# A decoder layer in split fp32: new start addresses, modulo 256 bytes, for the operands of the feed-forward matmuls

## The chip, the cores and the metric

The kernel runs as one program on one core of one Trainium2 chip. The metric is the time of one execution on the device, in microseconds (us). For the kernel before, the median of two runs is 1110.34 us (1110.25 and 1110.42).

## The reference

One decoder layer over 256 tokens of width 2048, in fp32. A mixer (attention over 8 heads beside a state-space branch) ends in a projection, a norm and a residual sum. Then comes the part that this case is about:

```python
h = rms_norm(x, ln_ffn_pre[l])
u = causal_depthwise_conv(h @ w_ffn_up[l], ffn_conv_w[l], ffn_conv_b[l])
gate, up = jnp.split(u, [FFN_HIDDEN], axis=-1)
f = (jax.nn.gelu(gate, approximate=True) * up) @ w_ffn_down[l]
x = x + rms_norm(f, ln_ffn_post[l])
```

`w_ffn_up` is 2048 x 11264 and `w_ffn_down` 5632 x 2048.

## The kernel before

**Split numbers.** A matmul in the fp32r type streams one column after the other but keeps fewer bits than fp32. So every operand is kept as two fp32r summands, `hi` and `lo` (the value minus `hi`), and a product is formed from three of the four partial products: hi*hi, hi*lo, lo*hi. TensorE (PE) does this work; everything else feeds it.

**Weights.** All weights come from HBM in units of 128 x 1024 fp32 (512 KB): 88 units of `win`, 32 of `wout`, and then twice 88 of `wup` and 44 of `wdown`. `Weights` (line 59) keeps them in rings. For each unit SyncE (SP) issues the load into a slot of `raw`, ScalarE (ACT) rounds it into a slot of `whi` (line 78) and VectorE (DVE) writes the difference into a slot of `wlo` (line 79). The rings of `whi` and `wlo` have 4 slots each in the pool `wp`; from the end of the mixer on, `deepen` adds 3 each in the pool `wq`. `tick` fetches one unit for each unit that PE has consumed.

**Projections by columns** (`cols_tile`, line 250, and `cols_part`, line 210), for the up projection: an output tile of 128 hidden columns by 256 tokens takes two units, each with 8 blocks of 128 x 128 weights. For each block `k` of the 16, the weights are the stationary operand and the activations `h2` the moving one, in a pair of matmuls:

```python
nc.tensor.matmul(ps, w[0][:, s], both, start=(k == 0), stop=False)
end[0] = nc.tensor.matmul(ps[:, c], w[1][:, s], hi, start=False, ...
```

The first (line 214) holds a block of `whi` and streams `both`, the two summands of `h2`, 2 x 256 columns; the second (line 215) holds the same block of `wlo` and streams the 256 columns of `hi`. Each loads its own stationary block (`LDWEIGHTS` in the profile's PEld rows). There are 88 such tiles; the first three of them (`held_up`) are worked in pieces by lines 223 and 226, so that 85 x 16 = 1360 pairs go by lines 214 and 215.

**Projections by rows** (`rows_chunk`, line 283, and `rows_part`, line 273), for the down projection: here a block of the gated activations `gT` is stationary and 512 columns of a weight unit stream. For each of the 22 blocks of a half, two token blocks and four chunks of 512 output columns there are three matmuls: `hi` with `whi` (line 278), `hi` with `wlo` (line 279), `lo` with `whi` (line 280), in all 6 x 176 = 1056 in the two halves.

**The feed-forward part** runs over two halves of the hidden width. In each half PE works 44 tiles of the up projection (22 gate tiles and 22 up tiles, in turn). ACT and DVE add the two halves of a finished sum in PSUM (`cols_sum`), apply the convolution, the GeLU and the product, and split the result into `gT` (`split_evac`). Then the four row chunks of the down projection over this half follow.

**Addresses.** SBUF addresses here are bytes within a partition, as the built program assigns them, and a residue is that address modulo 256. Every slot of `whi` and `wlo`, in `wp` and in `wq`, starts at residue 32. A block of 128 columns is 512 bytes and a chunk of 512 columns 2048, so every block and chunk in them starts at 32 as well. `normed` (line 340) makes `h2` as two planes, `lo` first, with 32 elements (128 bytes) beyond a plane's 4096: `lo` of each block `k` starts at 160 and `hi` at 32. `gT` is `[P, HALF, 2, S]` at residue 32, so every block of it, `hi` or `lo`, starts at 32. For the column projections of the mixer a shift (`SHIFT`, an argument of `units`) moves `wlo` by 128 bytes, to 160; there `hT` has its two summands side by side at 32. The row projections of the mixer have 32 against 32.

**Order.** The order on each engine is made by a scheduler from the order in which the code asks, its own estimates of when buffers come free, and the dependences.

Of the kernel before, what the change touches and what calls it, by code (L numbers as in the profile page):

```python
# [9 lines left out]
F32 = mybir.dt.float32  # L10
F32R = mybir.dt.float32r
# [3 lines left out]
ALU = mybir.AluOpType  # L15
# [4 lines left out]
P = 128  # L20
D = 2048
S = 256
# [7 lines left out]
HALF = NF // 2  # L30
# [3 lines left out]
UE = 1024  # L34
RELW = 384
RAWB = 4
SPLB = 4


SHIFT = 32  # L40
LOE = UE + 2 * SHIFT
HOLD = 5
MORE = {"raw": 0, "whi": 3, "wlo": 3}
WARM = 16
SIDE = 4

# [9 lines left out]
    return ap.bitcast(F32)  # L56


class Weights:

    def __init__(self, nc, pool, units):
        self.nc, self.pool, self.units = nc, pool, units
        self.fetched, self.ready, self.more, self.base, self.behind = 0, [], None, 0, 0

    def deepen(self, pool):

        self.more, self.base, self.behind = pool, self.fetched, MORE["whi"]

    def split(self, raw, hi, lo, i, s):
        self.rounded(raw, hi, lo, i, s)()
# [9 lines left out]
    def place(self, i, n, bufs, dtype):  # L82
        pool = self.pool
        if self.more and (i - self.base) % (bufs + MORE[n]) < MORE[n]:
            pool, bufs = self.more, MORE[n]
        wide = n == "wlo" and pool is self.pool
        return pool.tile([P, LOE if wide else UE], dtype, name=n, tag=n, bufs=bufs)
# [36 lines left out]
def decoder_layer(ctx, tc, x, xT, win, wdt, wout, wup, wdown, relb, vec, cols, mconv, fconv,  # L124
                  consts, out):
    nc = tc.nc
# [18 lines left out]
    def tok(t):  # L145
        return slice(t * P, (t + 1) * P)
# [63 lines left out]
    def cols_part(ps, w, aT, k, j):  # L210

        s = tok(j)
        both, hi, c = wide_and_hi(aT, k)
        nc.tensor.matmul(ps, w[0][:, s], both, start=(k == 0), stop=False)  # L214
        end[0] = nc.tensor.matmul(ps[:, c], w[1][:, s], hi, start=False,  # L215
                                  stop=(k == KT - 1)).ins

    def cols_tok(ps, w, aT, k, j, t):

        s = tok(j)  # L220
        both = ps.rearrange("p (b c) -> p b c", b=2)[:, :, tok(t)]
        c = k * S
        nc.tensor.matmul(both, w[0][:, s], aT[:, :, c:c + S][:, :, tok(t)],  # L223
                         start=(t == 0 and k == 0), stop=False)
        if t == NT - 1:
            nc.tensor.matmul(ps[:, S:], w[1][:, s], aT[:, 1, c:c + S], start=False,  # L226
                             stop=(k == KT - 1))

    def cols_sum(dst, ps):

        nc.scalar.copy(dst, ps[:, S:])
        nc.vector.tensor_tensor(dst, ps[:, :S], dst, op=ALU.add)

    pending, end = [], [None]

# [11 lines left out]
            with tc.issue_after(end[0]):  # L247
                fn(*args)

    def cols_tile(ps, aT):  # L250
        for u in range(2):
            w = ws.take()
            for j in range(8):
                cols_part(ps, w, aT, u * 8 + j, j)
            tick()

    def cols_first(pss, aT, after):
# [12 lines left out]
    def chunk_psums():  # L270
        return [acc.tile([P, 512], F32, name="pa", tag="a") for _ in range(NT)]
# [40 lines left out]
    def units(w, a, n, shift=0):  # L312
        return [(w[i], shift) for i in range(a, a + n)]

    ws = Weights(nc, wp, units(win, 0, 16, SHIFT) + units(win, 16, 16) + units(win, 32, 16, SHIFT)
                 + units(win, 48, 16) + units(win, 64, 24, SHIFT) + units(wout, 0, 32)
                 + [u for half in range(2)
                    for u in units(wup, half * 88, 88) + units(wdown, half * 44, 44)])
# [21 lines left out]
    def normed(name):  # L340

        return pers.tile([P, 2, KT * S + SHIFT], F32R, name=name, tag="h", bufs=1)

    def wide_and_hi(aT, k):

        if len(aT.shape) == 4:
            return aT[:, k, :, :], aT[:, k, 0, :], slice(0, S)
        c = slice(k * S, (k + 1) * S)
        return aT[:, :, c], aT[:, 1, c], slice(S, 2 * S)

    def summands(aT):

        if len(aT.shape) == 4:
            return [aT[:, :, c, :] for c in range(2)]
        return [aT[:, c, :KT * S].rearrange("p (k s) -> p k s", s=S) for c in (1, 0)]
# [5 lines left out]
    with ExitStack() as mctx:  # L361
# [3 lines left out]
        with ExitStack() as actx:  # L365
# [90 lines left out]
            rows = pers.tile([P, NT, SG, 8, P], F32, name="rows", tag="mm", bufs=1)  # L456
# [291 lines left out]
            lo, hi = range(8, KT, 2), range(0, 8, 2)  # L748
            first = [chunk_psums() for _ in range(2)]
# [25 lines left out]
        h2 = normed("h2")  # L775
# [38 lines left out]
        def turned(t, q):  # L814

            pt = psum("pxt").rearrange("p (j c) -> p j c", c=P)
            for j in range(4):
                nc.tensor.transpose(pt[:, j, :], ml[t][q][:, tok(j)], ident)
            dst = [d[:, q * 4:q * 4 + 4, tok(t)] for d in summands(h2)]
# [19 lines left out]
        both = list(lo) + list(hi)  # L839
# [111 lines left out]
    def summed(ps):  # L951
        u = fp.tile([P, S], F32, name="cfu", tag="cf", bufs=8)
        cols_sum(u, ps)
        return u

    def conv_ffn(f, u):
# [48 lines left out]
    def gated(i, ug, uu):  # L1005
        cg = conv_ffn(i, ug)
        nc.scalar.activation(cg, cg, AF.Gelu_apprx_tanh)
        cu = conv_ffn(NF + i, uu)
        k = i % HALF
        nc.vector.tensor_tensor(cu, cg, cu, op=ALU.mult)  # L1010
        split_evac(gT, k, slice(0, S), cu)

    held = []
    defer(5, lambda: along_tokens(rb2, [sums[:, t:t + 1] for t in range(NT)]))
    for half in range(2):
        for i in range(half * HALF, (half + 1) * HALF):
            ps = held_up[2 * i:2 * i + 2]
            for _ in range(2 - len(ps)):
                ps.append(col_psum())
                cols_tile(ps[-1], h2)  # L1020
            us = [summed(p) for p in ps]
            if i < 2:
                defer(5 - 2 * i, gated, i, *us)
            else:
                gated(i, *us)
        if half == 1:
            wpo = pers.tile([P, D], F32, name="wpo", tag="h", bufs=1)
            aux(out=wpo, in_=row_bcast(V_FFNPOST, D))
            nc.scalar.mul(wpo, wpo, -0.5)
        for c in range(4):  # L1030
            if half == 0 and c >= 2:
                held.append([psum("ph") for _ in range(NT)])
                rows_chunk(held[-1], gT, range(0, HALF, 2), last=False)
            elif half == 1 and c == 2:
                rows_chunk(held[0], gT, range(0, HALF, 2), first=False, done=fdone(1, c))
            elif half == 1 and c == 3:
                fearly += [early_sum(ss[2][t][:, :3]) for t in range(NT)]
                kts = range(0, HALF, 2)
                tail = rows_to_tail(held[1], gT, kts, first=False)
                for t in range(NT):  # L1040
                    for j in range(HOLD):
                        rows_tail(held[1], gT, kts, tail, t, j)
                    fdone(1, 3)(t, held[1][t])
            else:
                rows_chunk(chunk_psums(), gT, range(0, HALF, 2), done=fdone(half, c))


def _cols_units(w):
# [97 lines left out]
```

## Time and profile before

| | |
|---|---|
| median of the runs | 1110.34 us |
| the profiled execution, first to last instruction (its span) | 1107.4 us |
| the profiled execution as a whole, beside its span | not given by the profile; the median lies 2.9 us above the span |
| PE busy | 1100.1 us, 99% of the span |
| DVE, ACT busy | 784.0 us (71%), 592.3 us (53%) |
| granted TensorE clock, mean | 0.998 |
| matmuls by lines 214/215 with `h2` | 1360 + 1360 |
| matmuls by lines 278, 279, 280 with `gT` | 1056 |

The profile gives for each matmul a start and a modelled end. Matmuls overlap in the pipeline: a 128x512 one is shown as 0.39 us long, but the next one starts 0.23 us after it. So what a matmul costs is read from the distance between starts, which is called its pitch here, or from the count of matmuls in a window in which PE never waits. The times in a timeline are rounded to 0.01 us.

### The profile page before, as it was taken

Reading aid. Unit: us, or ns where it says so; the run is one execution under the profiler, and the core shown is the slowest. Engines: PE = TensorE matmul, PEld = TensorE weight load, DVE = VectorE, ACT = ScalarE, POOL = GpSimd, SP = SyncE. Lnnn points to the kernel's source line nnn. Section 1 sums busy time; section 2 is a strip of 40 time slices with the busy share of each in tenths; the row PEclk is TensorE's granted clock in tenths of the full one; section 3 lists DMA queues with packets and bytes.
Section 4 is the critical chain, followed back from the end, with each engine's and each line's share of the span. In section 5 each row is a group of like instructions: output and inputs, shape, how many; then the busy total and the mean of one; then the engine's idle time right before and its main releaser. Section 6 shows DMA issues by size and latency. Waiting matters only on the chain.

```text
span 1107.4 us, 15791 instructions
## 1 busy us (share of the span) xinstructions
PE 1100.1 (99%) x5888; PEld 945.1 (85%) x5888; DVE 784.0 (71%) x1270; ACT 592.3 (53%) x914; POOL 15.5 (1%) x26
## 2 busy tenths in 40 slices
PE   9999999999999999999999999999999999999997
PEld 7888888888888988888888888888888888888886
DVE  6698976776566899878787644448787878765553
ACT  6666545545454586555555444345555555554441
POOL 0010000000000000000000000000000000000000
PEclk9999999999999999999999999999999999999999
DMA  8857555555687267665556665565566565666652
GB/s 297 298 187 262 186 154 167 177 172 168 217 298 245 96 216 242 192 189 190 191 188 189 194 195 190 192 194 188 191 189 191 189 192 190 189 201 219 200 158 76
DMA packets 61356, 217.58 MB, mean 196 GB/s; under 512 B 7200, under 2 KB 8624, under 8 KB 60384
## 3 DMA queue, kind: packets, MB, share of 16 engines
q1 hardware_dynamic: 59328, 207.64, 58.3%
q0 software_dynamic: 1664, 8.59, 2.3%
q8 instruction: 46, 0.75, 0.3%
q10 hardware_dynamic: 288, 0.35, 0.1%
q14 instruction: 30, 0.25, 0.1%
HBM read 214.44 MB, written 2.11 MB: 196 GB/s over the span
## 4 chain that ended last, share of the span: by engine, by line
PE 99%; DMA 0%; SPq 0%; ACT 0%; issue 0%; DVE 0%; POOLq 0%; ACTq 0%
PE pa L214 36%; PE pa L215 18%; PE pa L278 9%; PE pa L280 9%; PE pa L279 9%; PE ph L280 4%; PE ph L279 4%; PE ph L278 4%; PE pab L214 1%; PE pa L223 1%; PE pab L215 1%; PE py L604 1%; PE pa L226 0%; PE pq L223 0%; DMA raw<-in_win_dram 0%; PE lg L694 0%
## 5 line engine op out<-in xcount | busy, mean ns | idle before, releaser
L79 DVE TENSOR_TENSOR wlo<-raw,whi 128x1024 fp32r<-128x1024 f32 (+2 forms) x389 | 469.7, 1210 | 249.0 <-ACT whi L78 240.9
L78 ACT CAST whi<-raw 128x1024 fp32r<-128x1024 f32 (+2 forms) x389 | 403.7, 1040 | 415.5 <-PE pa L214 193.3
L214 PE MATMUL pa<-h,whi 128*128 128x512 f32 x1360 | 471.7, 394 | 0.0
L215 PE MATMUL pa<-h,wlo 128*128 128x256 f32 x1360 | 379.4, 279 | 0.0
L214 PEld LDWEIGHTS pa<-h,whi 128*128 128x128 f32 x1360 | 255.7, 188 | 57.7
L215 PEld LDWEIGHTS pa<-h,wlo 128*128 128x128 f32 x1360 | 255.5, 188 | 0.0
L214 PE MATMUL pa<-hT,whi 128*128 128x512 f32 x384 | 136.5, 397 | 0.0
L215 PE MATMUL pa<-hT,wlo 128*128 128x256 f32 x384 | 107.0, 281 | 0.0
L214 PEld LDWEIGHTS pa<-hT,whi 128*128 128x128 f32 x384 | 72.1, 188 | 15.2 <-issue 0.2
L962 DVE SCALAR_TENSOR_TENSOR cfc<-cfu,fcv,cfc 128x254 f32<-128x254 f32 (+1 forms) x176 | 83.5, 479 | 1.4
L215 PEld LDWEIGHTS pa<-hT,wlo 128*128 128x128 f32 x384 | 72.1, 189 | 0.6 <-issue 0.2
L278 PE MATMUL pa<-whi,gT 128*128 128x512 f32 x176 | 68.6, 390 | 0.0
L280 PE MATMUL pa<-whi,gT 128*128 128x512 f32 x176 | 68.5, 389 | 0.0
L278 PE MATMUL ph<-whi,gT 128*128 128x512 f32 x176 | 68.5, 389 | 0.0
L279 PE MATMUL pa<-wlo,gT 128*128 128x512 f32 x176 | 68.5, 389 | 0.0
L279 PE MATMUL ph<-wlo,gT 128*128 128x512 f32 x176 | 68.5, 389 | 0.0
L280 PE MATMUL ph<-whi,gT 128*128 128x512 f32 x176 | 68.5, 389 | 0.0
L960 ACT ACTIVATE cfc<-cfu,fcv 128x256 f32<-128x256 f32 x88 | 52.3, 598 | 1.3 <-DVE cfu L959 1.3
L278 PE MATMUL pa<-whi,hT 128*128 128x512 f32 x128 | 51.2, 400 | 0.0
L278 PE MATMUL pa<-whi,mT 128*128 128x512 f32 x128 | 50.3, 393 | 0.0
L280 PE MATMUL pa<-whi,hT 128*128 128x512 f32 x128 | 50.1, 392 | 0.0
L279 PE MATMUL pa<-wlo,hT 128*128 128x512 f32 x128 | 50.0, 391 | 0.0
(230 smaller groups left out, 1131.6 us busy)
## 6 DMA issues: line engine op xcount, KB each, us to landing
raw<-in_wup_dram SPq DMA_DIRECT2D x176, 512.0 KB, 3.7
raw<-in_wdown_dram SPq DMA_DIRECT2D x88, 512.0 KB, 3.6
raw<-in_win_dram SPq DMA_DIRECT2D x85, 512.0 KB, 3.6
raw<-in_wout_dram SPq DMA_DIRECT2D x32, 512.0 KB, 3.9
xsq<-in_x_dram SPq DMA_DIRECT2D x2, 1024.0 KB, 10.3
rows<-acd POOLq DMA_DIRECT2D x4, 512.0 KB, 8.9
xt<-in_x_dram POOLq DMA_DIRECT2D x2, 1024.0 KB, 6.7
xr<-in_xT_dram SPq DMA_DIRECT2D x6, 256.0 KB, 6.4
```

The lines of the kernel that those rows point to most:

```text
L78: nc.scalar.copy(hi[:, s], raw[:, s])
L79: return lambda: nc.vector.tensor_tensor(lo[:, s], raw[:, s], f32(hi[:, s]), op=ALU.subtract)
L214: nc.tensor.matmul(ps, w[0][:, s], both, start=(k == 0), stop=False)
L215: end[0] = nc.tensor.matmul(ps[:, c], w[1][:, s], hi, start=False, stop=(k == KT - 1)).ins
L223: nc.tensor.matmul(both, w[0][:, s], aT[:, :, c:c + S][:, :, tok(t)], start=(t == 0 and k == 0), stop=False)
L278: nc.tensor.matmul(ps, a, w[0][:, s], start=(first and j == 0), stop=False)
L279: nc.tensor.matmul(ps, a, w[1][:, s], start=False, stop=False)
L280: end[0] = nc.tensor.matmul(ps, b, w[0][:, s], start=False, stop=(last and j == 1)).ins
L604: nc.tensor.matmul(py[:, i * 64:(i + 1) * 64], rows[:, t, g, i, :], xcs[t, g][:, i * 64:(i + 1) * 64], start=True, stop=True)
L960: nc.scalar.activation(c, u, AF.Identity, scale=wv[:, 2:3], bias=wv[:, 3:4])
L962: nc.vector.scalar_tensor_tensor(c[:, sh:], u[:, :S - sh], wv[:, 2 - sh:3 - sh], c[:, sh:], op0=ALU.mult, op1=ALU.add)
```

## The change

1. One tile `wx` takes the place of `whi` and `wlo`: 2 x 1024 elements, `hi` first. The rings keep 4 slots in `wp` and 3 in `wq`. For the units of `win` and `wout` (indices up to 119) the residues stay as they were.
2. For the units of `wup` and `wdown`, `hi` and `lo` together are moved by 0, 8, 24 or 56 elements (0, 32, 96, 224 bytes), if the slot is one of the four in `wp`; a slot in `wq` has no room for it (`room` is 0) and stays at 32. So these weights start at residue 32, 64, 128 or 0. In the up projection the step changes after every 8 units, in the down projection after every 2.
3. `h2`: the blocks `k` of a quarter (0-3, 4-7, 8-11, 12-15) are moved by 0, 4, 8, 16 elements (`at_k`). So `hi` starts at 32, 48, 64, 96 and `lo` 128 bytes beyond it.
4. `gT`: a block takes 2 x 256 + 16 elements and is moved by 0, 4, 8, 16 elements by `k` modulo 4, so that it starts at 32, 112, 192, 32 (and so on), `hi` and `lo` alike.

An option to hold `hi` and `lo` element by element ("pair") and one to run through them backwards (`back`) are in the code and not used. The arithmetic is the same.

```diff
+    def place(self, i):
+        if self.more and (i - self.base) % (SPLB + MORE) < MORE:
+            return self.more.tile([P, 2 * UE], F32R, name="wx", tag="wx", bufs=MORE), 0
+        return self.pool.tile([P, 2 * UE + 2 * SHIFT], F32R, name="wx", tag="wx", bufs=SPLB), 1
 
     def tiles(self, i):
-        raw = self.place(i, "raw", RAWB, F32)
-        hi, lo = (self.place(i, n, SPLB, F32R) for n in ("whi", "wlo"))
-        lo = lo[:, self.units[i][1]:][:, :UE]
...
+        elif i > 119:
+            w = w[:, shift * room:]
+            hi, lo = w[:, :UE], w[:, UE:][:, :UE]
+        else:
+            hi, lo = w[:, :UE], w[:, UE + shift:][:, :UE]
...
+    steps = (0, 8, 24, 56)
+
+    def up_units(i):
+        return units(wup, 4 * i, 4, steps[i // 2 % 4])
+
+    def down_units(half):
+        return [(wdown[half * 44 + i], "plane", steps[i // 2 % 4]) for i in range(44)]
...
+    def at_k(k):
+        o = k * S + (0, 4, 8, 16)[k // 4]
+        return slice(o, o + S)
...
-    gT = fp.tile([P, HALF, 2, S], F32R, name="gT")
+    gTs = fp.tile([P, HALF, 2 * S + 16], F32R, name="gT")
+    gT = [Spread([gTs[:, k, (0, 4, 8, 16)[k % 4]:] for k in range(HALF)])] * 2
```

PE has the same instructions in the same order in both programs. On ACT and DVE the single tile `wx` moves the roundings of weights by a place or two, since the scheduler reckons with one tile for both summands. On ACT, in the middle of the second half of the up projection, where `cfu` is the sum taken out of PSUM, `cfc` the convolution and `gT` the gated result, there stands before:

```order
705 L201 CAST gT<-cfc 128x256 [waits DVE_49]
706 L231 COPY cfu<-pa 128x256 [waits PE_49]
707 L78 CAST whi<-raw 128x1024 [waits DMAHW7_49,PE_49]
708 L78 CAST whi<-raw 128x1024 [waits DMAHW0_49,PE_49]
709 L231 COPY cfu<-pa 128x256 [waits PE_49]
710 L960 ACTIVATE cfc<-cfu,fcv 128x256 [waits DVE_49]
711 L78 CAST whi<-raw 128x1024 [waits DMAHW1_49,PE_49]
```

and, at the same place, in the changed kernel (its lines 97, 228, 262 and 1009 are the old 78, 201, 231 and 960):

```order
703 L97 CAST wx<-raw 128x1024 [waits DMAHW5_49,PE_49]
704 L97 CAST wx<-raw 128x1024 [waits DMAHW6_49,PE_49]
705 L228 CAST gT<-cfc 128x256 [waits DVE_49]
706 L262 COPY cfu<-pa 128x256
707 L97 CAST wx<-raw 128x1024 [waits DMAHW7_49,PE_49]
708 L262 COPY cfu<-pa 128x256 [waits PE_49]
709 L1009 ACTIVATE cfc<-cfu,fcv 128x256 [waits DVE_49]
```

One rounding of weights, which waits for PE to release its slot, now stands ahead of the rounding of `gT` and the copy `cfu` instead of behind them. The number of roundings per tile is the same.

More of the change, by code (lines that the diff above doesn't have):

```diff
@@ L40 @@
 SHIFT = 32
-LOE = UE + 2 * SHIFT
 HOLD = 5
-MORE = {"raw": 0, "whi": 3, "wlo": 3}
+MORE = 3
 WARM = 16
@@ L56, in f32, with __init__, summand, __getitem__ @@
     return ap.bitcast(F32)
+class Spread:
+    def __init__(self, rows):
+        self.rows = rows
+    def summand(self, c):
+        return Part(self.rows, c)
+class Part:
+    def __init__(self, rows, c):
+        self.rows, self.c = rows, c
+    def __getitem__(self, at):
+        _, k, ts = at
+        return self.rows[k][:, self.c * S:(self.c + 1) * S][:, ts]
 class Weights:
@@ L67, in deepen @@
     def deepen(self, pool):
-        self.more, self.base, self.behind = pool, self.fetched, MORE["whi"]
+        self.more, self.base, self.behind = pool, self.fetched, MORE
     def split(self, raw, hi, lo, i, s):
@@ L80, in rounded @@
                                                op=ALU.subtract)
[L82 to L87, printed above, removed]
-    def tiles(self, i):
-        raw = self.place(i, "raw", RAWB, F32)
-        hi, lo = (self.place(i, n, SPLB, F32R) for n in ("whi", "wlo"))
-        lo = lo[:, self.units[i][1]:][:, :UE]
+    def place(self, i):
+        if self.more and (i - self.base) % (SPLB + MORE) < MORE:
+            return self.more.tile([P, 2 * UE], F32R, name="wx", tag="wx", bufs=MORE), 0
+        return self.pool.tile([P, 2 * UE + 2 * SHIFT], F32R, name="wx", tag="wx", bufs=SPLB), 1
+    def tiles(self, i):
+        raw = self.pool.tile([P, UE], F32, name="raw", tag="raw", bufs=RAWB)
+        w, room = self.place(i)
+        _, layout, shift = self.units[i]
+        if layout[:4] == "pair":
+            w = w[:, shift * room:][:, :2 * UE]
+            hi, lo = (w.rearrange("p (c z) -> p z c", z=2)[:, z, :] for z in range(2))
+        elif i > 119:
[3 more added lines that the diff above has]
+            hi, lo = w[:, :UE], w[:, UE + shift:][:, :UE]
+        if layout[-1] == "-":
+            hi, lo = hi[:, ::-1], lo[:, ::-1]
         self.ready.append((hi, lo))
@@ L248, in tick, with cols_tile @@
                 fn(*args)
-    def cols_tile(ps, aT):
+    def cols_tile(ps, aT, back=False):
         for u in range(2):
@@ L310, in rows_tail, with units @@
         rows_part(pss[t], tail[j], aT, kts[len(kts) - HOLD + j], t, False, j == HOLD - 1)
-    def units(w, a, n, shift=0):
-        return [(w[i], shift) for i in range(a, a + n)]
+    def units(w, a, n, shift=0, layout="plane"):
+        return [(w[i], layout, shift) for i in range(a, a + n)]
+    steps = (0, 8, 24, 56)
[3 more added lines that the diff above has]
+        return [(wdown[half * 44 + i], "plane", steps[i // 2 % 4]) for i in range(44)]
     ws = Weights(nc, wp, units(win, 0, 16, SHIFT) + units(win, 16, 16) + units(win, 32, 16, SHIFT)
@@ L317, in decoder_layer @@
                  + [u for half in range(2)
-                    for u in units(wup, half * 88, 88) + units(wdown, half * 44, 44)])
+                    for u in [u for i in range(22 * half, 22 * half + 22) for u in up_units(i)]
+                    + down_units(half)])
     cstt = pers.tile([P, 2 * P + SH], F32, name="cst")
@@ L347, in wide_and_hi @@
             return aT[:, k, :, :], aT[:, k, 0, :], slice(0, S)
-        c = slice(k * S, (k + 1) * S)
+        c = at_k(k)
         return aT[:, :, c], aT[:, 1, c], slice(S, 2 * S)
     def summands(aT):
+        if isinstance(aT, Spread):
+            return [aT.summand(c) for c in range(2)]
         if len(aT.shape) == 4:
@@ L818, in turned @@
                 nc.tensor.transpose(pt[:, j, :], ml[t][q][:, tok(j)], ident)
-            dst = [d[:, q * 4:q * 4 + 4, tok(t)] for d in summands(h2)]
+            o = at_k(q * 4).start
+            dst = [h2[:, c, o:o + 4 * S].rearrange("p (k s) -> p k s", s=S)[:, :, tok(t)]
+                   for c in (1, 0)]
             last = [nc.scalar.copy(dst[0], pt).ins]
@@ L1017, in decoder_layer @@
             ps = held_up[2 * i:2 * i + 2]
+            back = False
             for _ in range(2 - len(ps)):
                 ps.append(col_psum())
-                cols_tile(ps[-1], h2)
-            us = [summed(p) for p in ps]
+                cols_tile(ps[-1], h2, back)
+            us = [summed(p, back) for p in ps]
             if i < 2:
@@ L1032, in decoder_layer @@
                 held.append([psum("ph") for _ in range(NT)])
-                rows_chunk(held[-1], gT, range(0, HALF, 2), last=False)
+                rows_chunk(held[-1], gT[half], range(0, HALF, 2), last=False)
             elif half == 1 and c == 2:
-                rows_chunk(held[0], gT, range(0, HALF, 2), first=False, done=fdone(1, c))
+                rows_chunk(held[0], gT[half], range(0, HALF, 2), first=False, done=fdone(1, c))
             elif half == 1 and c == 3:
@@ L1038, in decoder_layer @@
                 kts = range(0, HALF, 2)
-                tail = rows_to_tail(held[1], gT, kts, first=False)
+                tail = rows_to_tail(held[1], gT[half], kts, first=False)
                 for t in range(NT):
                     for j in range(HOLD):
-                        rows_tail(held[1], gT, kts, tail, t, j)
+                        rows_tail(held[1], gT[half], kts, tail, t, j)
                     fdone(1, 3)(t, held[1][t])
             else:
-                rows_chunk(chunk_psums(), gT, range(0, HALF, 2), done=fdone(half, c))
+                rows_chunk(chunk_psums(), gT[half], range(0, HALF, 2), done=fdone(half, c))
 def _cols_units(w):
```

26 lines of the change are left out of this document (15 added, 11 removed).

## The prediction

> **What bounds the kernel now.** I read the head of the page first, then the waits of PE, then the counts of matmuls in windows, and the timeline last.
>
> ```profile
> span 1107.4 us, 15791 instructions
> PE 1100.1 (99%) x5888; PEld 945.1 (85%) x5888; DVE 784.0 (71%) x1270; ACT 592.3 (53%) x914; POOL 15.5 (1%) x26
> PE pa L214 36%; PE pa L215 18%; PE pa L278 9%; PE pa L280 9%; PE pa L279 9%; PE ph L280 4%; PE ph L279 4%; PE ph L278 4%; PE pab L214 1%; PE pa L223 1%; PE pab L215 1%; PE py L604 1%; PE pa L226 0%; PE pq L223 0%; DMA raw<-in_win_dram 0%; PE lg L694 0%
> ```
>
> ```profile
> engine line waited for: us in total, times, longest us
> PE pa L996 <- ACT diag L994: 1.6, 1, 1.6
> PE idle L335 <- DVE junk L332: 1.1, 1, 1.1
> PE pab L214 <- ACT whi L78: 0.3, 1, 0.3
> ```
>
> The chain that ended last is PE itself, and PE waits 3.0 us in all (1.6 + 1.1 + 0.3), none of it in the feed-forward part. So the time is the number of matmuls times their pitch, and a change of addresses counts only if it changes the pitch of matmuls or makes PE wait. The counts, and four windows that lie wholly in the up projection (the first two) and in the down projection (the last two):
>
> ```profile
> L214 PE MATMUL pa<-h,whi 128*128 128x512 f32 x1360 | 471.7, 394 | 0.0
> L215 PE MATMUL pa<-h,wlo 128*128 128x256 f32 x1360 | 379.4, 279 | 0.0
> L278 PE MATMUL pa<-whi,gT 128*128 128x512 f32 x176 | 68.6, 390 | 0.0
> L278 PE MATMUL ph<-whi,gT 128*128 128x512 f32 x176 | 68.5, 389 | 0.0
> ```
>
> ```profile
> core 0: us, PE busy (x) PEld busy (x) DVE busy (x) ACT busy (x) POOL busy (x), PEclk, DMA share, GB/s
> 410.00:610.00 200.00, 200.00 (x1155) 175.54 (x1154) 163.00 (x267) 119.18 (x190) 0.00 (x0) 1.00 0.62 195
> 740.00:950.00 210.00, 210.00 (x1213) 184.28 (x1213) 163.98 (x263) 121.21 (x188) 0.00 (x0) 1.00 0.60 190
> 625.00:725.00 100.00, 100.00 (x443) 82.86 (x442) 45.17 (x37) 40.73 (x41) 0.00 (x0) 1.00 0.61 194
> 985.00:1085.00 100.00, 100.00 (x442) 82.83 (x442) 51.53 (x53) 43.71 (x50) 0.00 (x0) 1.00 0.55 182
> ```
>
> Of the 1155 matmuls, one had begun before its window: 200 / 1154 = 0.1733 us each, or 0.3465 us for a pair of lines 214 and 215 (210 / 1212 gives the same). In the row projection a matmul of 512 columns takes 100 / 442 = 0.2262 us. The granted clock is 1.00 in all four. Lines 279 and 280 have as many as 278, so there are 6 x 176 = 1056 of those.
>
> **How much of the pitch could depend on addresses.** A plain fp32 matmul shows what a column costs when the array is fed at a slower rate. Line 611 streams 512 columns in two passes:
>
> ```profile
> 169.60 1.02 PE L611 MATMUL po<-xd,cross 128*128 128x512 f32 x2
> 170.46 0.49 PE L717 MATMUL ppt<-cst,pm 128*128 128x128 f32 x3
> ```
>
> Two passes take 0.86 us, 0.43 us each. I take this as two clocks per column, with a load of weights hidden beside it, so that 512 fp32r columns at one clock would take 0.215 us and a pair of 768 columns 0.3225 us (an estimate from these rows). What the fp32r matmuls take beyond that is then 0.2262 - 0.215 = 0.0112 us in the row projection, with one load of weights per matmul, and 0.3465 - 0.3225 = 0.024 us in the up projection, with two. It goes with the loads and not with the columns: 11 to 12 ns for each load. So the stream and the load beside it disturb each other a little, and this is the whole sum that addresses can act on: 1360 x 0.024 = 32.6 us and 1056 x 0.0112 = 11.8 us, together 44.4 us, 4% of the time.
>
> The Trainium skill, in "TensorE: Matmul & The Clock Gate", Part 2, says that PE has two independent read ports into SBUF, so that loading the next weights takes no read bandwidth from the running matmul. By that rule residues change nothing. The 11 ns per load are not what it would lead one to expect, though no run here shows yet that they have to do with addresses.
>
> **Do the rows of before show a residue that costs more?** There are three pairings of stream and load. In the row projection it is 32 against 32: 0.2262 us. In the up projection the first matmul streams 160 and then 32 and the load beside it starts at 32; in the second it is 32 against 32: 0.3465 us a pair. In the mixer's column projections the load during the first matmul starts at 160 instead:
>
> ```profile
> 24.82 0.39 PE L214 MATMUL pab<-hT,whi 128*128 128x512 f32 x1
> ...
> 25.86 0.39 PE L214 MATMUL pa<-hT,whi 128*128 128x512 f32 x1
> ```
>
> ```profile
> 126.76 0.39 PE L214 MATMUL pa<-hT,whi 128*128 128x512 f32 x1
> ...
> 128.16 0.39 PE L214 MATMUL pa<-hT,whi 128*128 128x512 f32 x1
> ```
>
> Three pairs in 1.04 us are 0.347 each, four in 1.40 are 0.350: the same residues, two values. And within the up projection, with one set of residues, pairs alternate:
>
> ```profile
> 501.30 0.40 PE L214 MATMUL pa<-h,whi 128*128 128x512 f32 x1
> 501.53 0.28 PE L215 MATMUL pa<-h,wlo 128*128 128x256 f32 x1
> 501.65 0.39 PE L214 MATMUL pa<-h,whi 128*128 128x512 f32 x1
> 501.88 0.28 PE L215 MATMUL pa<-h,wlo 128*128 128x256 f32 x1
> 501.99 0.40 PE L214 MATMUL pa<-h,whi 128*128 128x512 f32 x1
> 502.23 0.28 PE L215 MATMUL pa<-h,wlo 128*128 128x256 f32 x1
> 502.35 0.39 PE L214 MATMUL pa<-h,whi 128*128 128x512 f32 x1
> ```
>
> A short pair takes 0.34 us, and with the window's mean a long one 2 x 0.3465 - 0.34 = 0.353. Block and chunk starts are the same modulo 256 in both kinds, so the difference is one of timing: what a load costs depends on when it meets the stream. Why would the mean be the same for every residue? A load takes 0.11 us:
>
> ```profile
> 122.81 0.97 PEld L604 LDWEIGHTS py<-xc,rows 128*128 128x128 f32 x8
> ```
>
> Eight loads in 0.97 us, the last one 0.19 us long as modelled, are (0.97 - 0.19) / 7 = 0.11 us apart, beside matmuls of only 64 columns. In that time a load reads 512 bytes per partition, and the stream, at 2048 bytes in 0.2262 us, 996. Their distance runs through 484 bytes, nearly two turns of 256. Whatever residues they start from, they meet at all distances; a start moves only the moment of the meeting. That is my reason for a forecast near zero. It assumes that a load reads evenly through its 0.11 us, which no row shows.
>
> **The change part by part.**
>
> Mixer, 0 to 387 us: the residues of the `win` and `wout` units, `hT` and `mT` are unchanged, 0 us.
>
> Up projection, 1360 pairs: new distances, with changes every 4 blocks (`h2`) and from slot to slot (weights). Bounds: all pairs like the short one, 1360 x 0.0065 = -8.8 us; all like the long one, +8.8 us. What I take lies between, a little above zero, since a break in the rhythm costs something. After the matmuls of line 226, which have another shape, the first five pairs took
>
> ```profile
> 387.71 0.39 PE L214 MATMUL pa<-h,whi 128*128 128x512 f32 x1
> ...
> 389.46 0.39 PE L214 MATMUL pa<-h,whi 128*128 128x512 f32 x1
> ```
>
> 1.75 us, 0.350 each instead of 0.3465. Were the rhythm never to settle, this would be 1360 x 0.0035 = 4.8 us; I take half of that, +2.4 us, as residues change after every fourth block.
>
> Down projection, 1056 matmuls: at 0.2262 us in both halves, 0 us taken. Bounds per load from the two kinds of pair: (0.34 - 0.3225) / 2 = 0.0088 and (0.353 - 0.3225) / 2 = 0.0153 us instead of 0.0112, so -2.5 to +4.3 us.
>
> One tile for both summands: a slot is released by the last read of either, one matmul later (at most 0.12 us by the rows above), while a unit lasts 8 pairs, 2.77 us, and 7 slots stand ready: 0 us. ACT is told to round one unit earlier in its order, so `gT` and `cfu` stand behind a wait for PE:
>
> ```profile
> ACT whi L78 <- PE pa L214: 180.3, 154, 1.7
> ```
>
> They come at most 1.7 us later. A tile lasts 5.5 us and has four PSUM buffers, so PE asks for a buffer again after four tiles and never waits for it in the rows above: 0 us. If that cover were gone, it would be 1.7 us for every other tile, 42 x 1.7 = 71 us. DMAs and their queue are unchanged.
>
> Sum: 1107.4 + 2.4 = 1109.8 us of span. The median of the runs lies 2.9 us above the span (1110.34 - 1107.4), which makes 1112.7, so 1113 us. The bounds together, -8.8 - 2.5 and +8.8 + 4.3, give this case 1099 to 1123.
>
> "SBUF — State Buffer" of the Trainium skill, section "Door 1: The DMA port swizzle", has lines of 16 bytes, with a cost for each crossing into a new line. All new shifts are multiples of 16 bytes, so by that rule no operand crosses more lines than before, and the sum is the same by it.
>
> **The rivals.**
>
> *No effect at all.* The 11 ns are a fixed cost of exchanging weights, blind to addresses: 1110.3 us, the median as it is. For it: three pairings, one cost per load. Against it: short and long pairs under the same instructions, and plain fp32 passes that hide it. The rule of the two ports, from the page of the Trainium skill named above, stands with this case.
>
> *Faster.* The old residues, 32 or 160 everywhere, could be an unlucky choice, as both are the same modulo 128, and other distances could let a load pass unharmed. All of it gone would be -44.4 us, 1066. Since three of seven slots stay at 32, 4/7 of it is the likelier price: -25.4 us, 1085. Against it: the distance runs round anyway.
>
> *Slower.* Where a load happens to advance at the pace of the stream for part of its time, their distance stands still, and a bad start then costs all through that part. At the old distances, 0 and 128, this may be absent. Its place is both projections; it costs over 2%, 22.2 us, from 22.2 / (2 x 1360 + 1056) = 5.9 ns more per load, half again as much as now. Twice the cost in 4/7 of the slots is +25.4 us, 1136; in all, through `h2` and `gT`, which shift against the slots that stay, 1155. For it: the long pair shows 15 ns per load, so more than 11 is possible. Against it: no residue of before is bad.
>
> That the change does not do what it says can be half true: slots in `wq` do not move. But 3 of 4 quarters of `h2` do, so most distances are new.
>
> **How the numbers follow.** My forecast, distances that even out with a little unrest, 0.46, at 1113; no effect 0.25; faster 0.12, of which 0.08 beyond 2%; slower 0.17, of which 0.14 beyond 2%. About 2% (22 us) is what a measurement of this kernel can tell from no change. So faster 0.08, same 0.78, slower 0.14. The range has to reach into both rivals, to where some 0.08 to 0.1 is left on each side: 1090 to 1134, by the centres 1085 and 1136 of the two. My likeliest case alone has 1099 to 1123.
>
> **What would show it.** Windows in the up projection of the changed profile should give pairs of 0.340 to 0.353 us, in the down projection 0.224 to 0.230 us per matmul; a pair near 0.33 or a matmul near 0.22 would be the faster rival, a pair from 0.359 (0.3465 + 2 x 0.0059) the slower one. Sorted by the quarter of `h2`, pitches that differ by more than 10 ns would mean that a start does matter. The rows of PE's waits should still show nothing in the feed-forward part; a wait of PE for `cfu` or `wx` would mean that the order of ACT and not the addresses made the difference. The mixer should end at 387 us as now.

## The result

The changed kernel takes 1119.91 us (median of two runs, 1119.38 and 1120.44) against 1110.34 us. The ratio is 1.0088, with a 95% interval from 1.0059 to 1.0117: 9.6 us slower, under the 2% of the stated chances. The profiled execution has a span of 1118.4 us against 1107.4.

The head of its page, and PE's waits:

```profile
span 1118.4 us, 15776 instructions
PE 1111.0 (99%) x5888; PEld 948.1 (85%) x5888; DVE 785.1 (70%) x1270; ACT 592.7 (53%) x914; POOL 15.6 (1%) x26
```

```profile
PE pa L1045 <- ACT diag L1043: 1.6, 1, 1.6
PE idle L375 <- DVE junk L372: 1.1, 1, 1.1
PE pa L310 <- DVE wx L98: 0.3, 1, 0.3
```

The same 5888 matmuls, the same 3.0 us of waiting, and PE is busy 10.9 us longer. So the time is in the pitch. Windows in the changed kernel (the first number in brackets is the count of matmuls), the first two in the up projection and the last two in the down projection:

```profile
410.00:610.00 200.00, 200.00 (x1146) 174.78 (x1145) 161.74 (x265) 119.07 (x189) 0.00 (x0) 1.00 0.64 192
745.00:955.00 210.00, 210.00 (x1203) 183.63 (x1202) 162.67 (x259) 119.50 (x187) 0.00 (x0) 1.00 0.62 188
625.00:735.00 110.00, 110.00 (x476) 89.16 (x475) 49.02 (x41) 43.87 (x45) 0.00 (x0) 1.00 0.61 190
990.00:1100.00 110.00, 110.00 (x476) 89.11 (x475) 54.18 (x56) 45.00 (x52) 0.00 (x0) 1.00 0.55 173
```

and two of the kernel before that are as long as the last two:

```profile
620.00:730.00 110.00, 110.00 (x487) 91.15 (x486) 51.28 (x45) 45.06 (x47) 0.00 (x0) 1.00 0.61 194
985.00:1095.00 110.00, 110.00 (x487) 91.10 (x487) 53.29 (x58) 44.40 (x52) 0.56 (x1) 1.00 0.50 165
```

In 110 us PE starts 476 row matmuls where it started 487, at a clock of 1.00 in all. A window also counts the one or two that had begun before it; from the starts of the first and the last matmul of a stage, the exact pitches are

| | before | changed |
|---|---|---|
| a pair of the up projection | 0.3467 us | 0.3497 us |
| a matmul of the down projection | 0.2267 us | 0.2320 us |

The starts of the stages give the account. Of before, the first matmul of the first down projection, of the second up projection, of the second down projection, and the last one (the first full pair is in the prediction, at 387.71):

```profile
615.36 0.39 PE L278 MATMUL pa<-whi,gT 128*128 128x512 f32 x1
...
735.06 0.40 PE L214 MATMUL pa<-h,whi 128*128 128x512 f32 x1
...
979.13 0.39 PE L278 MATMUL pa<-whi,gT 128*128 128x512 f32 x1
...
1098.61 0.39 PE L280 MATMUL ph<-whi,gT 128*128 128x512 f32 x1
```

Of the changed kernel, from the first full pair on:

```profile
389.03 0.40 PE L243 MATMUL pa<-h,wx 128*128 128x512 f32 x1
...
618.70 0.40 PE L309 MATMUL pa<-wx,gT 128*128 128x512 f32 x1
...
741.17 0.40 PE L243 MATMUL pa<-h,wx 128*128 128x512 f32 x1
...
987.40 0.40 PE L309 MATMUL pa<-wx,gT 128*128 128x512 f32 x1
...
1109.64 0.39 PE L311 MATMUL ph<-wx,gT 128*128 128x512 f32 x1
```

Up projection: 229.67 - 227.65 = +2.0 and 246.23 - 244.07 = +2.2 us. Down projection: 122.47 - 119.70 = +2.8 and 122.24 - 119.48 = +2.8 us. Together +9.7 us (unrounded); the medians differ by 9.6. The mixer is 1.3 us later in this one execution; that is no effect of residues, as the first experiment shows.

### The profile page after: what moved, and what is told of

Same layout as the page of the kernel before. It is cut to its first block, busy times and chain, and to the rows that moved or that the text cites. A ratio compares the mean times of both kernels' runs of the same rounds, so it can differ in the third digit from the quotient of the medians.

```text
span 1118.4 us, 15776 instructions
## 1 busy us (share of the span) xinstructions
PE 1111.0 (99%) x5888; PEld 948.1 (85%) x5888; DVE 785.1 (70%) x1270; ACT 592.7 (53%) x914; POOL 15.6 (1%) x26
## 4 chain that ended last, share of the span: by engine, by line
PE 96%; DMA 1%; SPq 0%; ACT 0%; DVE 0%; issue 0%; POOLq 0%; ACTq 0%
PE pa L243 36%; PE pa L244 18%; PE pa L309 8%; PE pa L310 8%; PE pa L311 8%; PE ph L309 4%; PE ph L310 4%; PE ph L311 4%; PE pab L243 1%; DMA raw<-in_wout_dram 1%; PE pa L251 1%; PE py L650 1%; DMA raw<-in_win_dram 1%; PE pab L244 1%; PE pq L251 0%
## 5 line engine op out<-in xcount | busy, mean ns | idle before, releaser
L98 DVE TENSOR_TENSOR wx<-raw,wx 128x1024 fp32r<-128x1024 f32 (+2 forms) x389 | 469.4, 1209 | 224.9 <-ACT wx L97 223.9
L97 ACT CAST wx<-raw 128x1024 fp32r<-128x1024 f32 (+2 forms) x389 | 402.6, 1037 | 356.5 <-PE pa L244 128.2
L243 PE MATMUL pa<-h,wx 128*128 128x512 f32 x1360 | 475.9, 395 | 0.0
L244 PE MATMUL pa<-h,wx 128*128 128x256 f32 x1360 | 381.1, 280 | 0.0
L243 PEld LDWEIGHTS pa<-h,wx 128*128 128x128 f32 x1360 | 255.4, 188 | 59.7
L244 PEld LDWEIGHTS pa<-h,wx 128*128 128x128 f32 x1360 | 256.2, 188 | 0.0
L243 PE MATMUL pa<-hT,wx 128*128 128x512 f32 x384 | 137.1, 399 | 0.0
L244 PE MATMUL pa<-hT,wx 128*128 128x256 f32 x384 | 107.4, 282 | 0.0
L243 PEld LDWEIGHTS pa<-hT,wx 128*128 128x128 f32 x384 | 72.6, 189 | 15.4 <-issue 0.2
L244 PEld LDWEIGHTS pa<-hT,wx 128*128 128x128 f32 x384 | 72.5, 190 | 0.7 <-DVE wx L98 0.2
L310 PE MATMUL pa<-wx,gT 128*128 128x512 f32 x176 | 69.5, 395 | 0.0
L310 PE MATMUL ph<-wx,gT 128*128 128x512 f32 x176 | 69.5, 395 | 0.0
L309 PE MATMUL pa<-wx,gT 128*128 128x512 f32 x176 | 69.5, 395 | 0.0
L309 PE MATMUL ph<-wx,gT 128*128 128x512 f32 x176 | 69.4, 394 | 0.0
L311 PE MATMUL pa<-wx,gT 128*128 128x512 f32 x176 | 69.3, 394 | 0.0
L311 PE MATMUL ph<-wx,gT 128*128 128x512 f32 x176 | 69.3, 394 | 0.0
```

The lines of the kernel that those rows point to most:

```text
L97: nc.scalar.copy(hi[:, s], raw[:, s])
L309: nc.tensor.matmul(ps, a, w[0][:, s], start=(first and j == 0), stop=False)
L310: nc.tensor.matmul(ps, a, w[1][:, s], start=False, stop=False)
L311: end[0] = nc.tensor.matmul(ps, b, w[0][:, s], start=False, stop=(last and j == 1)).ins
```

## The experiments

The diffs stand against the changed kernel. In experiments 5 to 11 the weights' residues and the spread of the blocks are also taken out, as in the first one; what the diffs show comes on top of that. A line of three dots marks what is left out. Experiments 5 to 11 were timed once each, and those not given below took 1113.69 us (experiment 7), 1113.98 (8) and 1127.02, 1122.58 and 1117.82 (9 to 11), the kernel before beside them 1110.1 to 1110.7. "Distance" means the residue of the stream minus that of the load beside it, modulo 256. Pitches in the tables are worked out from the starts in the trace, sorted by the residues that the built program gives to each matmul.

**1. The tile without the residues.**

```diff
-    steps = (0, 8, 24, 56)
+    steps = (0, 0, 0, 0)
...
-        o = k * S + (0, 4, 8, 16)[k // 4]
+        o = k * S
...
-    gTs = fp.tile([P, HALF, 2 * S + 16], F32R, name="gT")
-    gT = [Spread([gTs[:, k, (0, 4, 8, 16)[k % 4]:] for k in range(HALF)])] * 2
+    gTs = fp.tile([P, HALF, 2 * S], F32R, name="gT")
+    gT = [Spread([gTs[:, k, :] for k in range(HALF)])] * 2
```

> The one tile for both summands is kept, with the order on ScalarE and VectorE that comes of it; every residue is as before. Three theories. Unrest (what costs is that the distance between stream and load keeps changing, so that the rhythm of the matmuls never settles): 1110.3 us, pairs 0.3465 us, row matmuls 0.2262 us. Bad starts (certain distances cost more, held or not): the same. Order (the moved roundings and the shared slot make the difference): about 1119.9 us.

Measured: 1109.87 us, ratio 0.9999 (0.9990 to 1.0009). Pairs 0.3467, row matmuls 0.2267 us. The order theory falls: the moved roundings and the shared slot cost nothing. Its mixer ends late as well, with all residues as before, while its time is that of before (in experiments 2 to 4, 7, 8 and 12 the same point lies between 387.8 and 388.9 us):

```profile
388.61 0.39 PE L243 MATMUL pa<-h,wx 128*128 128x512 f32 x1
```

**2 to 4. One part of the change alone.** Each undoes two of the three edits shown above.

> Only the gated activations take other residues (32, 112, 192, 32 by block). Unrest: row matmuls 0.2315 us as in the changed kernel, 1056 x 0.0052 = +5.5 us, so 1115.8 us; blocks that stay at 32 rise as much as the others. Bad starts: the same sum at most, but loads at 32 against a stream at 32 stay at 0.2262 us and only the loads at 112 and 192 rise. Order: as the run with the tile alone.

> Only the second norm's activations take other residues, by quarter of k. Unrest: pairs near 0.349 us in all four quarters, the unmoved first quarter too, 1360 x 0.0025 = +3.4 us, so about 1113.7 us; rows 0.2262 us. Bad starts: the first quarter, whose distances are those of before, stays at 0.3465 us, the other three rise to 0.350 or more.

> Only the up and down weights take other residues, in four of seven slots. Unrest: small, since a distance is now held for at least 8 pairs in the up projection (pairs 0.347 to 0.348 us, +1 to +2 us) and 12 matmuls in the rows (0.227 to 0.229 us, +1 to +3 us): 1112 to 1115 us. Bad starts: units in the unmoved slots stay at 0.3465 and 0.2262 us, moved ones rise to 0.352 and 0.2325 us, about +7 us: 1117 us.

| run | time, us | ratio to before | pair | row matmul |
|---|---|---|---|---|
| gated activations alone | 1114.88 | 1.0045 (1.0028 to 1.0062) | 0.3467 | 0.2317 |
| norm's activations alone | 1112.78 | 1.0022 (1.0011 to 1.0034) | 0.3490 | 0.2267 |
| weights alone | 1114.67 | 1.0041 (1.0026 to 1.0056) | 0.3474 | 0.2298 |

The kernel before took 1110.01 us on the same chip. Each part costs, and their sum, 4.87 + 2.77 + 4.66 = 12.3 us, is more than the 9.6 of all three: the rows are at 0.2317 us with the gated activations alone and at 0.2320 with everything. The gated activations alone, in the down projection, and the norm's activations alone, in the up projection:

```profile
625.00:735.00 110.00, 110.00 (x477) 89.05 (x476) 48.86 (x40) 43.46 (x44) 0.00 (x0) 1.00 0.58 190
410.00:610.00 200.00, 200.00 (x1148) 175.05 (x1147) 161.92 (x264) 118.93 (x190) 0.00 (x0) 1.00 0.60 192
```

With the gated activations alone, loads at 32 beside a stream at 32 took 0.2314 us on average, as much as those at 112 (0.2314); those at 192 took 0.2329. That is what the unrest theory said. With the weights alone, where a unit holds its residue for 12 matmuls, it is the other way round: units at 32 took 0.2273, those at 0, 64 and 128 took 0.2334, 0.2335 and 0.2338. The timeline of that run, at the first matmul of two units and of those that follow them:

```profile
677.56 0.40 PE L309 MATMUL ph<-wx,gT 128*128 128x512 f32 x1
...
680.36 0.40 PE L309 MATMUL ph<-wx,gT 128*128 128x512 f32 x1
...
688.61 0.39 PE L309 MATMUL ph<-wx,gT 128*128 128x512 f32 x1
...
691.33 0.39 PE L309 MATMUL ph<-wx,gT 128*128 128x512 f32 x1
```

Twelve matmuls of a unit at 0 took 2.80 us, 0.2333 each; twelve of one at 32 took 2.72, 0.2267. A moved unit does not settle to the old pitch. After a moved unit, the first three matmuls of one at 32 still took 0.2311 us on average, the next three 0.2297, the seventh 0.2278, and from the eighth on 0.2267. So distances have prices of their own, and the favourable one needs some seven matmuls to take hold. For the norm's activations the unmoved quarter was at 0.3475 us, the others at 0.3486, 0.3513 and 0.3484.

**5 and 6. Distances held through a stage.** The rings are made 4 + 2 slots so that every slot has room, and each of eight stages gets one shift (`ups` and `downs`, eight numbers each). The mixer runs slower with that ring (PE waits 4.2 us in it), so only the pitches count here, not the totals of 1126.01 and 1126.21 us.

```diff
-MORE = 3
+MORE = 2
...
-            return self.more.tile([P, 2 * UE], F32R, name="wx", tag="wx", bufs=MORE), 0
+            return self.more.tile([P, 2 * UE + 2 * SHIFT], F32R, name="wx", tag="wx", bufs=MORE), 1
...
-        return units(wup, 4 * i, 4, steps[i // 2 % 4])
+        return units(wup, 4 * i, 4, ups[i * 4 // 22])
...
-        return [(wdown[half * 44 + i], "plane", steps[i // 2 % 4]) for i in range(44)]
+        return [(wdown[half * 44 + i], "plane", downs[half * 4 + i // 11]) for i in range(44)]
```

> Activations as before; every weight slot has room, and the shift of the weights is held through a whole stage: in the up projection eight stages of about ten tiles with 16, 48, 64, 80, 112, 144, 176, 208 bytes, in the down projection eight chunks of 132 matmuls with 16, 48, 80, 112, 144, 176, 208, 240 bytes (the rings have 4 and 2 slots instead of 4 and 3). Unrest: a held distance settles, 0.2267 us per row matmul and 0.3465 us per pair in every stage. Bad starts: each stage has a pitch of its own; only the old distance (0 in the rows) gave 0.2267 in the run with the weights alone, the others 0.233, so about 0.233 us in all eight chunks, and 0.346 to 0.351 us per pair. A chunk under 0.224 us would be a better place than that of before.

> The same with other held shifts: 4, 8, 24, 32, 96, 128, 192, 224 bytes in the up projection, 4, 8, 24, 64, 128, 160, 192, 224 in the down projection. Unrest: 0.2267 us and 0.3465 us in every stage. Bad starts: 224 bytes gives the 0.2333 us that the run with the weights alone showed for a stream at 0 against a load at 32; shifts under a line of 16 bytes (4, 8) are nearest to the old place and stay near 0.2267 us if the distance counts in lines; pairs at 32, 96 and 224 bytes as in the run with the weights alone, 0.350, 0.347 and 0.348 us.

Row matmuls in nanoseconds, by the bytes by which the weights (the stream) were moved, the load at 32 as before; the value at 0 is that of before:

| 0 | 4 | 8 | 16 | 24 | 48 | 64 | 80 | 112 |
|---|---|---|---|---|---|---|---|---|
| 226.7 | 237.3 | 232.2 | 231.7 | 233.4 | 233.3 | 233.3 | 231.1 | 231.1 |

| 128 | 144 | 160 | 176 | 192 | 208 | 224 | 240 |
|---|---|---|---|---|---|---|---|
| 232.4 | 233.2 | 234.2 | 233.3 | 233.4 | 234.7 | 233.3 | 233.3 |

Pairs, by the bytes by which the weights (here the loads) were moved:

| 0 | 8 | 48 | 64 | 96 | 128 | 192 | 144, 176, 208, 224 | 32, 112 | 24 | 80 | 4 | 16 |
|---|---|---|---|---|---|---|---|---|---|---|---|---|
| 346.7 | 346.7 | 346.7 | 346.7 | 346.7 | 346.7 | 346.7 | 348.9 | 350.0 | 351.1 | 352.0 | 353.3 | 354.6 |

The unrest theory falls: 132 matmuls at one distance do not settle to 226.7 ns. In the rows every distance other than 0 costs 4.4 to 10.6 ns more. In the up projection six of the shifts cost nothing and the others 2 to 8 ns; none is below what the kernel before has. Two windows of the first of these runs, with the loads moved by 48 and by 80 bytes:

```profile
450.00:500.00 50.00, 50.00 (x290) 44.05 (x290) 39.95 (x65) 29.05 (x46) 0.00 (x0) 1.00 0.60 190
570.00:620.00 50.00, 50.00 (x286) 43.41 (x286) 39.53 (x66) 28.65 (x46) 0.00 (x0) 1.00 0.61 185
```

290 matmuls against 286 in the same 50 us.

**7. The gated activations held elsewhere, and half a load.**

```diff
-    gTs = fp.tile([P, HALF, 2 * S + 16], F32R, name="gT")
-    gT = [Spread([gTs[:, k, (0, 4, 8, 16)[k % 4]:] for k in range(HALF)])] * 2
+    gTs = fp.tile([P, HALF, 2 * S + 64], F32R, name="gT")
+    gT = [Spread([gTs[:, k, o:] for k in range(HALF)]) for o in (20, 0)]
+    gT[1].n = P // 2
...
-            nc.tensor.matmul(ps, a, w[1][:, s], start=False, stop=False)
+            n = getattr(aT, "n", P)
+            nc.tensor.matmul(ps[:n], a[:, :n], w[1][:, s], start=False, stop=False)
```

> In the first half all blocks of the gated activations stand at 112, the weights at 32: a distance of 176 bytes held through 528 matmuls, no change from block to block. Unrest: 0.2267 us. Bad starts: about 0.233 us, more than the 0.2317 us of the run in which the activations alone change from block to block, and the same as the chunk with the weights moved by 176 bytes. In the second half everything stands at 32, and the lines that multiply hi by wlo load only 64 of the 128 columns (that product is left out for the other 64 tokens of each block). If the 0.0117 us per load come from the bytes that a load reads, the matmuls beside which such a load runs go down by about 0.006 us to 0.221 us, and the others stay at 0.2267; if it is a fixed cost of exchanging weights, all stay at 0.2267 us.

The windows of the two halves:

```profile
625.00:735.00 110.00, 110.00 (x476) 89.02 (x475) 49.02 (x40) 43.09 (x44) 0.00 (x0) 1.00 0.59 191
990.00:1100.00 110.00, 110.00 (x480) 81.32 (x480) 53.24 (x57) 44.30 (x52) 0.57 (x1) 1.00 0.49 159
```

Measured: 232.0 ns with the blocks held at 112, as much as in the changed kernel, so again no settling to 226.7. The chunk whose weights were moved by 176 has the same distance and took 233.3 ns, so the distance alone does not give the pitch. In the second half the matmuls beside a half load took 228.8 ns, those that use it 230.5 and the third kind 230.0: none went down, all went up. Both readings offered for the load fall.

**8. Smaller loads everywhere in the rows.**

```diff
-            nc.tensor.matmul(ps, a, w[0][:, s], start=(first and j == 0), stop=False)
-            nc.tensor.matmul(ps, a, w[1][:, s], start=False, stop=False)
-            end[0] = nc.tensor.matmul(ps, b, w[0][:, s], start=False,
+            n = P if first and j == 0 else getattr(aT, "n", P)
+            nc.tensor.matmul(ps[:n], a[:, :n], w[0][:, s], start=(first and j == 0), stop=False)
+            n = getattr(aT, "n", P)
+            nc.tensor.matmul(ps[:n], a[:, :n], w[1][:, s], start=False, stop=False)
+            n = P if last and j == 1 else n
+            end[0] = nc.tensor.matmul(ps[:n], b[:, :n], w[0][:, s], start=False,
...
+    gT[0].n, gT[1].n = 32, 64
```

> All residues as before. The row matmuls of the down projection load 32 of the 128 columns in the first half and 64 in the second (the products for the other tokens of each block are left out, except in the first and last matmul of a chunk); the streams of 512 columns are unchanged. If the 0.0117 us over 0.215 us come from the bytes of the load: 0.218 us in the first half, 0.221 us in the second. If they are a cost of each matmul whatever it loads: 0.2267 us in both.

The windows of the two halves:

```profile
625.00:735.00 110.00, 110.00 (x477) 52.52 (x476) 49.01 (x40) 43.23 (x44) 0.00 (x0) 1.00 0.57 191
990.00:1100.00 110.00, 110.00 (x480) 64.63 (x479) 53.15 (x57) 44.17 (x52) 0.56 (x1) 1.00 0.47 159
```

The loads are shorter: busy time of PEld falls from 91.15 us to 52.52 and 64.63 us. The pitch rises, to 231.5 ns with 32 columns and 230.0 ns with 64. So what a matmul takes beyond its columns does not go down with the bytes of the load beside it. The edit narrows the output of each matmul along with its load, and no run separates the two.

**9 to 11. Is it the distance, the residue, or the step between blocks?** In three runs the stream and the load of the rows were moved by the same bytes, `o` elements, and the blocks of `gT` were `n` elements apart; the lines of the second run are shown.

```diff
+    gTs = fp.tile([P, HALF * (2 * S + 64)], F32R, name="gT")
+    gT = [Spread([gTs[:, o + k * n:] for k in range(HALF)]) for o, n in ((8, 512), (20, 512))]
```

> Down projection: stream and load moved by the same amount, both at 112 in the first half and both at 48 in the second, so that their distance is 0 as before. If the distance modulo 256 is what counts: 0.2267 us in both halves. If the residue 32 itself is what counts: 0.231 to 0.234 us, as with 16 or 80 bytes between them. Up projection, eight held stages: the lo weights alone moved by 64, 128, 192, 48 bytes, then the hi weights alone by 64, 128, 192, 48. If each load counts by its own distance, pairs differ between the two groups; if only the settled rhythm counts, values between 0.3465 and 0.355 us come again, none below. A stage under 0.344 us would be a better place than that of before.

> The run that moved stream and load of the row matmuls alike also took the blocks of the gated activations 2304 bytes apart instead of 2048, and gave 0.2333 us. Here the blocks are 2048 bytes apart as before, and both are at 64 in the first half and at 112 in the second. Distance: 0.2267 us in both halves, so that the step between blocks was the cause there. Residue 32 itself: 0.233 us in both. Distance, but only in steps of 32 bytes: 0.2267 and 0.2333 us. Up projection: the norm's activations at 64 (hi) and 192 (lo), eight held weight shifts; with 32 bytes the distances are those of before, and by the distance theory pairs take 0.3467 us there.

> First half: everything at 32 as before, but the blocks of the gated activations 2304 bytes apart. If only residues modulo 256 count: 0.2267 us; if the step between blocks counts: about 0.233 us. Second half: blocks 2048 apart, stream and load both at 160. Distance: 0.2267 us. Residue 32 itself: about 0.233 us. Up projection: mostly unmoved, 0.3467 us per pair.

| stream and load both at | blocks apart, bytes | row matmul, ns |
|---|---|---|
| 32 | 2304 | 226.7 |
| 64 | 2048 | 226.7 |
| 160 | 2048 | 226.7 |
| 48 | 2304 | 233.3 |
| 112 | 2304 | 233.3 |
| 112 | 2048 | 233.3 |

The windows of the run with 64 in the first half and 112 in the second:

```profile
630.00:740.00 110.00, 110.00 (x487) 91.09 (x486) 50.43 (x44) 45.20 (x46) 0.00 (x0) 1.00 0.59 192
1000.00:1110.00 110.00, 110.00 (x473) 88.60 (x473) 55.42 (x60) 43.30 (x52) 0.56 (x1) 1.00 0.49 160
```

and of the run with the blocks 2304 bytes apart in the first half and both operands at 160 in the second:

```profile
630.00:740.00 110.00, 110.00 (x487) 91.13 (x486) 50.39 (x44) 45.52 (x46) 0.00 (x0) 1.00 0.60 192
990.00:1100.00 110.00, 110.00 (x487) 91.09 (x486) 56.25 (x61) 46.46 (x54) 0.00 (x0) 1.00 0.55 179
```

The step between blocks does not count at a residue of 32, nor is that residue the only good one. Among the starts tried, the rows have the low pitch only at a distance of 0, and there a common move by 32 or 128 bytes keeps it while one by 16 or 80 loses it: the third reading in the expectation, steps of 32 bytes. In the up projection, with the norm's activations moved by 32 bytes, the weights moved by 32 too gave 346.7 ns, as before. The other seven stages, with weights at 0, 32, 96, 128, 160, 192 and 224 beside activations whose `hi` lies at 64, gave 346.7 to 350.0 ns in six and 353.3 in one, and runs without the common move gave the same for the same distances. So there, too, a common move by 32 bytes changes nothing; one by 16 was not tried.

In the first of these three runs the `lo` or the `hi` weights of the up projection were moved alone. Moving `lo` alone by 48, 64, 128 and 192 bytes gave 353.3, 350.0, 346.7 and 351.1 ns, moving `hi` alone 346.8, 350.0, 350.0 and 351.6. With `lo` at 64 the first two tiles of the stage took 346.8 ns a pair, and only the later ones 350.0. Both loads count, and no stage was under 346.7. The third run moved both weights by two more distances, with the norm's activations as before: 160 bytes gave 353.3 ns and 240 gave 346.7.

**12. The row part undone.**

```diff
-        return [(wdown[half * 44 + i], "plane", steps[i // 2 % 4]) for i in range(44)]
+        return units(wdown, half * 44, 44)
...
-    gTs = fp.tile([P, HALF, 2 * S + 16], F32R, name="gT")
-    gT = [Spread([gTs[:, k, (0, 4, 8, 16)[k % 4]:] for k in range(HALF)])] * 2
+    gTs = fp.tile([P, HALF, 2 * S], F32R, name="gT")
+    gT = [Spread([gTs[:, k, :] for k in range(HALF)])] * 2
```

> The changed kernel with only its row part undone: gated activations and down weights at 32 again; the norm's activations and the up weights as changed. If each row matmul's extra comes from its own stage and the up projection's from its own: rows 0.2267 us, pairs 0.3497 us as in the changed kernel, 1360 x 0.003 = +4.1 us, so 1114.2 us. If the parts act on each other across stages: not this sum.

Measured: 1114.05 us, ratio 1.0036 (1.0023 to 1.0049), where 1114.2 was expected. A window of its up projection and one of its down projection:

```profile
410.00:610.00 200.00, 200.00 (x1145) 174.79 (x1144) 161.58 (x264) 118.69 (x190) 0.00 (x0) 1.00 0.61 192
625.00:735.00 110.00, 110.00 (x487) 91.09 (x486) 50.23 (x42) 44.32 (x44) 0.00 (x0) 1.00 0.60 196
```

The first has the count of the changed kernel (1146), the second that of before (487). The two parts add up stage by stage.

No version faster than before came out of the 17 distances tried in the rows and the 19 tried in the pairs, 0 included; the kernel before sits at the lowest pitch seen in both.

## Why the prediction was right and wrong

**What bounds the kernel: right.** PE never waits in the feed-forward part before or after, and the whole difference is pitch.

**One tile for both summands, and the moved roundings: right at 0** (1109.87 us with them alone). The mixer at 0 was right as well.

**Up projection, +2.4 us: the size was off.** It measured +4.2 us (2.0 + 2.2). It lies inside the bounds of 8.8 either way. The row for unrest, 0.350 us for pairs after a break, was near what came, 0.3497, and it was the halving of it that had no row behind it. But the nearness is partly chance, as held distances, without any break, cost up to 8 ns more as well. The sign that the prediction set for a start that matters, quarters of `h2` more than 10 ns apart, was too coarse: in the changed kernel they lie between 348.8 and 350.4 ns.

**Down projection, 0 us: wrong, and outside its bounds.** It measured +5.5 us where the bounds were -2.5 to +4.3. This is the term that makes most of the miss from 1113 to 1119.9. The bounds came from the two kinds of pair in the up projection, by way of an extra per load; the rows go their own way, with 231 to 237 ns at every distance held but 0. That the total still fell between 1099 and 1123 us was partly luck: the up projection stayed well below its own bound, which left room for this excess.

**"They meet at all distances": wrong.** That stream and load pass through nearly all distances, and that a start therefore only shifts the meeting, was the reason for a forecast near zero. Held through 132 matmuls, 16 other distances gave 231 to 237 ns in the rows and only 0 gave 226.7 (where the common residue was 32, 64 or 160). The rows of before could not show it, as all row projections of that kernel have distance 0. The argument was about a mean over distances, but the matmuls settle into a rhythm that goes with the two starts.

**"It goes with the loads": wrong.** That rows had one load and 11 ns, and pairs two loads and 24 ns, fitted just as well with so much per matmul. Loads of a quarter of the size, with outputs as much narrower, did not lower the pitch (231.5 ns). What the time over 215 ns is spent on stays open; that load and stream act on each other is shown by the distances.

**No effect at all: refuted** by each of the runs with one part. The rule of two independent ports ("TensorE: Matmul & The Clock Gate", Part 2, of the Trainium skill) does not cover this: 232 against 227 ns, by nothing but the addresses of stream and load.

**Slower: the mechanism that came nearest.** Its point, that the old distance is a good one and that some others cost more for as long as they are held, is what the held stages show. Its price was too high: it doubled an extra of 11 ns in 4/7 of the slots, +25.4 us, and what the moved distances cost is 5 ns in the rows and 3 ns a pair, +9.7 us. Its picture of a load that advances at the pace of the stream was not tested.

**Lines of 16 bytes.** The cost of each crossing into a new line of 16 bytes ("SBUF — State Buffer", "Door 1: The DMA port swizzle", of the Trainium skill) was no guide here. By it the prediction took shifts by multiples of 16 bytes as free, but a common move by 16 bytes costs 6.6 ns in each row matmul and one by 32 costs none.

The count in a window was read a little off in the prediction (0.2262 for 0.2267 us), since a window counts, besides the matmuls that start in it, one or two that had begun before: 441 start in 100 us, not 442.

## What to carry to other kernels

In this kernel, where PE is busy throughout and streams fp32r, the start of the moving operand relative to that of the stationary operand loaded beside it is worth a few per cent of the matmul's pitch: 226.7 against 231 to 237 ns for 512 columns. At a distance of 0 the common start counts too: 226.7 or 233.3 ns. If the trace of a kernel shows one distance only, it says nothing about the others, however steady it is; hold each distance through a stage of a hundred matmuls or so, many in one run, and read the pitches. Mixing distances gave no average of good and bad here, since the good one needs several matmuls to take hold.

## What was not expected of the hardware

Settled rhythms repeat on a grid of 6.67 ns. The second half of the rows with both operands at 48, first and last matmul:

```profile
993.53 0.40 PE L309 MATMUL pa<-wx,gT 128*128 128x512 f32 x1
...
1116.50 0.39 PE L311 MATMUL ph<-wx,gT 128*128 128x512 f32 x1
```

and the first half of the rows with both at 64:

```profile
624.05 0.40 PE L309 MATMUL pa<-wx,gT 128*128 128x512 f32 x1
...
743.53 0.39 PE L311 MATMUL ph<-wx,gT 128*128 128x512 f32 x1
```

Each holds 528 matmuls (3 lines x 176), so 122.97 / 527 = 0.2333 and 119.48 / 527 = 0.2267 us. They differ by 6.7 ns, and 226.7 and 233.3 are 34 and 35 times 6.67 ns; the settled pairs, 346.7 and 353.3 ns, are 52 and 53 times that, and the short pair of the prediction, 340 ns, 51 times. Other values come from rhythms of several matmuls, as with the short and long pairs: with the stream moved by 80 bytes (231.1 ns) the pitches repeat as 230, 235 and 228 ns, three matmuls in 104 steps of 6.67 ns, and with 128 bytes (232.4 ns) seven matmuls take 244 steps. What the step of 6.67 ns is, no run here shows.

With smaller loads beside them, and outputs as much narrower, the streams were slower and not faster: 231.5 ns with 32 columns and 230.0 with 64, against 226.7 with 128, all at the favourable distance.
